# The tokens of each expert pair gathered by two fp32r matmul passes in place of one fp32 pass, in a fused two-block transformer kernel

## The chip, the cores and the metric

One core of a Trainium2 chip runs the whole kernel. The metric is device time in microseconds (us) for one execution. TensorE is called PE below, its weight loads PEld, VectorE DVE, ScalarE ACT, GpSimd POOL, and SyncE, which issues nearly all loads, SP.

## The reference, cut to what matters

Two transformer blocks in a row on 256 tokens of width 1024, all in float32. The first ends in a mixture of experts: every token picks one of 4 groups and two of the group's 4 experts.

```
g_sel = argmax(t @ w_rg + b_rg)                       # one group a token
top_p, top_i = top_k(softmax(e_logits[g_sel]), 2)     # two experts in it
combine[t, g, e] = one_hot(g_sel) * g_w * within      # 256 x 4 x 4, 2 nonzero a row
hid = silu(t @ w_gate[e]) * (t @ w_up[e])             # 1024 -> 512, 16 experts
y   = sum_e (hid * combine[:, e]) @ w_down[e]         # 512 -> 1024
```

The second block is a gated mixer with attention and a convolutional feed-forward part of width 2816; the change doesn't touch its arithmetic.

## The kernel before, in words

The kernel runs as one program, in this order: modulation and attention of block 1, its output projection, the router, eight steps over pairs of experts (`for p in range(8)`), a branch for the rare case that an expert has more than 64 tokens, and block 2. The order of PE's instructions is the order in which the code is written; the other engines are ordered by a scheduler.

**Number formats on PE.** A matmul of float32 operands stands in the trace as two records, each with a weight load of its own. Most products of the kernel are made instead from operands that are split into a high and a low part of type fp32r (`halves`, `mm3`, L332 to L334): a matmul of fp32r operands is one record with one weight load. For the experts' own matrices the kernel uses float32 (L1072, L1073, L1118, L1119).

**The expert step.** An expert's tokens are put into 64 slots. `slots_of` (L980 to L985) makes the 0/1 matrix `SS[p]` of a pair on DVE: for each of two blocks of 128 tokens a row per token, and 2 x 64 slots. `gather` (L1054 to L1062) multiplies it with the tokens: `hT` (tokens as rows, 1024 features, float32) gives the weights, 128 features at a time, and `SS[p]` the 128 moving columns. Eight feature tiles by two token blocks are 16 float32 matmuls a pair, which fill two PSUM banks. ACT and DVE in turn scale and shift each tile into `XE` (`affine`, L1050 and L1052). Then come, on PE: the gate matmuls (`pairmm(pg, 0)`, two experts beside each other in the two halves of the array's columns), two transposes of `SS[p]` and two small matmuls that fetch the combine weights (L1082, L1084), the up matmuls, `combine` of the pair before (L1027, L1028: fp32r, from `yH`, `yL` and the transposed 0/1 matrix `ST`), four transposes of the hidden values (L1106), the gather of the next pair, and the down matmuls. `gather(0)` stands ahead of the loop, right behind the router.

**Loads.** The expert matrices come as 96 chunks of 1 MB, in the order of their use, all on SP's queue (`moe_next`, L839 and L292). `KIND` names, for the first chunks in turn, the pool that lends the buffer: 0 `rawp`, 1 `big`, 2 `bigB`, 3 `wp`, 4 the tile `tL` of `ho`. The list has 21 entries, so 21 chunks can be on their way or unused at once; chunk n waits for the last reader of chunk n - 21. The first loads of block 2 (`in_wC`) follow on the same queue; `raw0` (L1169) is the first of them. It is split by ACT (L1176) and by DVE and POOL (L1179). At the branch (L1129) all engines meet.

Of the kernel before, what the change touches and what calls it, by code (L numbers as in the profile page):

```python
# [9 lines left out]
F32 = mybir.dt.float32  # L10
F32R = mybir.dt.float32r
I32 = mybir.dt.int32
AF = mybir.ActivationFunctionType
OP = mybir.AluOpType
# [3 lines left out]
P = 128  # L18
D = 1024
# [5 lines left out]
CAP = 64  # L25
# [91 lines left out]
LAG = 2  # L117
DELAY_FROM = NF - 2
LASTCUT = 94
KIND = [1] * 9 + [0, 0, 1, 0, 0, 2, 2, 2, 3, 3, 4, 1]  # L120
FIRST = "m0 m1 w0 w3"
WARM = 30
EARLY = ("x0 j4 g0 x1 r0 c0 s0 h0 pA g1 j1 c1 h1 pB A0 g2 A1 c2 h2 g3 B0 B1 c3 h3 A2 B2 pC g4 C0 C1 B3 c4 g5 h4 A3 C2 A4 c5 h5 B4 C3 g6 A5 c6 g7 h6 B5 C4 l0 A6 c7 h7 "
# [86 lines left out]
def build(tc, xT, cT, consts, constsA, constsZ, vec, wmod, wA, relb, wE, wC, sgw, sgb, sgln, gfin, out, dbg=None):  # L210
    nc = tc.nc
    vat = VEC_AT
    cat, catA, catZ = [c.at for c in _consts()]
    mm = nc.tensor.matmul
# [6 lines left out]
    with ExitStack() as top:  # L221
# [5 lines left out]
        wp = pool(top, "wp", bufs=WPB)  # L227
        pool(top, "gapH").tile([P, 16], F32, name="gapH")
        ho = pool(top, "ho")
# [31 lines left out]
        ident = cst("ident")  # L261
# [15 lines left out]
        def follow(d, e):  # L277
            tc.add_manual_dep(d.ins, e.ins.name, order_only, reason="first things first")
# [10 lines left out]
        def load(src, n=2048, pl=None, cuts=1):  # L289
            t = (pl or rawp).tile([P, 2048], F32, name=nm_("raw"), tag="raw")  # L290
            for a, b in pieces(n, cuts):
                queue(nc.sync.dma_start(t[:, a:b], src[:, a:b]))  # L292
            return t
# [69 lines left out]
        with ExitStack() as sa:  # L363
            ap = pool(sa, "ap")
            big = pool(sr, "big", bufs=BIG, side="right")

            def bigt(shape, name, dt=F32):
                n = int(np.prod(shape[1:]))
                t = big.tile([P, 2048], dt, name=name, tag="raw")
                t = t[:shape[0], :n]  # L370
                if len(shape) == 3:
                    return t.rearrange("p (a b) -> p a b", a=shape[1])
                if len(shape) == 4:
                    return t.rearrange("p (a b c) -> p a b c", a=shape[1], b=shape[2])
                return t
# [42 lines left out]
            with ExitStack() as sp:  # L418
# [14 lines left out]
                sqs_, d = [], silu  # L433
                for i, src in enumerate((X, CX)):
                    sq = bigt([P, KD, T], f"sq{i}")
                    sqs_.append(sq)
                    for k in range(0, KD, 2):
                        e = nc.scalar.activation(sq[:, k:k + 2], src[:, k:k + 2], AF.Square)
                        follow(e, d)
                        d = e  # L440
# [6 lines left out]
                col = pp.tile([P, 4], F32, name="colA")  # L447
# [81 lines left out]
                for step in EARLY.split():  # L529
                    f, k = step[0], step[1]  # L530
# [3 lines left out]
                    k = int(k)  # L534
# [66 lines left out]
                ps = proj(ch[1], 0, 512, 64)  # L601
# [227 lines left out]
            def moe_next():  # L829
                i = moe_q[0]  # L830
                moe_q[0] += 1
                n = i - len(KIND)
                kind = KIND[i % len(KIND)]
                if kind == 0:
                    return load(moe_chunk(i), cuts=2 if i >= LASTCUT else 1)
                pl, tag = {1: (big, "raw"), 2: (bigB[-1], "raw"), 3: (wp, "w"), 4: (ho, "tL")}[kind]
                t = pl.tile([P, 2048], F32, name=nm_("raw"), tag=tag)
                for a, b in pieces(2048, 2 if i >= LASTCUT else 1):
                    d = queue(nc.sync.dma_start(t[:, a:b], moe_chunk(i)[:, a:b]))  # L839
                    tc.add_manual_dep(d.ins, (used[n] if n >= 0 else moe_gate[0]).ins.name, complete, reason="prefetch")  # L840
                return t
# [81 lines left out]


        with sb:
            def small(shape, name, dt=F32):
                return bp.tile([P] + shape, dt, name=name)

            def bc(ap_, n):
                return ap_.unsqueeze(len(ap_.shape)).to_broadcast(list(ap_.shape) + [n])  # L930
# [14 lines left out]
            nc.vector.tensor_reduce(mx_, L, axis=AX.X, op=OP.max)  # L945
            nc.vector.tensor_sub(L, L, bc(mx_, 4))
            lexp[0] = nc.scalar.activation(ex, L, AF.Exp)
            hT = ho.tile([P, 2, D], F32, name="hT", tag="tH")
            for g in range(2):
                for b in range(2):  # L950
                    follow(nc.scalar.activation(hT[:, b, g * 512:(g + 1) * 512], tks[g, b], AF.Copy, scale=col[:, b:b + 1]), lexp[0])
            e1 = small([2, 5, 4], "e1")
            nc.vector.scalar_tensor_tensor(e1, L, 0.0, prio, op0=OP.is_ge, op1=OP.mult)
            nc.vector.tensor_reduce(mx_, e1, axis=AX.X, op=OP.max)
# [23 lines left out]
            SS = {}  # L978

            def slots_of(p):  # L980
                SS[p] = mix[:, 1536 + p % 2 * 256:1792 + p % 2 * 256].rearrange("p (b e s) -> p b e s", b=2, e=2)
                for b in range(2):
                    nc.vector.tensor_tensor(SS[p][:, b], bc(place[:, b, 2 * p:2 * p + 2], CAP),
                                            slot.unsqueeze(1).to_broadcast([P, 2, CAP]), op=OP.is_equal)
                SS[p] = SS[p].rearrange("p b e s -> p b (e s)")  # L985

            slots_of(0)
            comb = small([2, 4, 4], "comb")
            nc.vector.tensor_mul(comb, exe, top)
            den = small([2, 5], "den")  # L990
# [63 lines left out]
            def gather(p):  # L1054
                for g in range(2):
                    ps = bank()
                    for k in range(4):
                        for b in range(2):
                            d = (4 * g + k) * P
                            mm(ps[:, k * P:(k + 1) * P], hT[:, b, d:d + P], SS[p][:, b], start=b == 0, stop=b == 1)  # L1060
                    for k in range(4):
                        affine(XE[:, 4 * g + k], ps[:, k * P:(k + 1) * P], 4 * g + k, k % 2)  # L1062

            gather(0)
            for p in range(8):
# [13 lines left out]
                pairmm(pg, 0)  # L1079
                aux = bank()  # L1080
                for b in range(2):
                    nc.tensor.transpose(aux[:, b * P:(b + 1) * P], SS[p][:, b], ident)  # L1082
                for b in range(2):
                    mm(aux[:, 256:272], SS[p][:, b], comb[:, b], start=b == 0, stop=b == 1)  # L1084
                ST = br.tile([P, T], F32R, name=f"ST{p}", tag="ST")
                nc.vector.tensor_copy(ST, aux[:, :T])
                wt = br.tile([P, 1], F32, name=f"wt{p}", tag="wt")
# [39 lines left out]
                if p == 6:  # L1127
                    last[0] = None
                    with tc.If(n_most > CAP):  # L1129
                        spare = [bigB[-1].tile([P, 2048], F32, name=f"spare{c}", tag="raw") for c in range(3)]  # L1130
                        H2f, fw = spare[0].rearrange("p (k t) -> p k t", k=KD), spare[1:]
                        for k in range(KD):
                            ps = bank()
                            for b in range(2):
                                nc.tensor.transpose(ps[:, b * P:(b + 1) * P], hT[:, b, k * P:(k + 1) * P], ident)
                            affine(H2f[:, k], ps[:, :T], k, False)
                        hc = bigt([P, 5, T], "hc")
                        hid, cr = hc[:, 0:4], hc[:, 4]
                        with tc.For_i(0, NE, 1) as e:
                            nc.gpsimd.dma_start(cr, ovD[bass.ds(e, 1)].to_broadcast([P, T]))  # L1140

                            def dload(c):
                                t = fw[c % 2]
                                nc.sync.dma_start(t, wE[bass.ds(e, 1), c].rearrange("o p n -> p (o n)"))
                                return t
                            wg = [dload(0), dload(1)]
                            for f in range(4):
                                pg = bank()
                                for k in range(KD):
                                    s = slice((k % 4) * 512 + f * P, (k % 4) * 512 + (f + 1) * P)  # L1150
                                    mm(pg[:, :T], wg[k // 4][:, s], H2f[:, k], start=k == 0, stop=k == KD - 1)
                                nc.scalar.activation(hid[:, f], pg[:, :T], AF.Silu)
                            wu = [dload(2), dload(3)]
                            for f in range(4):
                                pu = bank()
                                for k in range(KD):
                                    s = slice((k % 4) * 512 + f * P, (k % 4) * 512 + (f + 1) * P)
                                    mm(pu[:, :T], wu[k // 4][:, s], H2f[:, k], start=k == 0, stop=k == KD - 1)
                                nc.vector.tensor_mul(hid[:, f], hid[:, f], pu[:, :T])
                                nc.vector.tensor_mul(hid[:, f], hid[:, f], cr)  # L1160
                            wd = [dload(4), dload(5)]
                            for m in range(KD):
                                ps = bank()
                                for f in range(4):
                                    s = slice((f % 2) * D + m * P, (f % 2) * D + (m + 1) * P)
                                    mm(ps[:, :T], wd[f // 2][:, s], hid[:, f], start=f == 0, stop=f == 3)
                                nc.vector.scalar_tensor_tensor(X[:, m], ps[:, :T], mod2[:, 24 + m:25 + m], X[:, m], op0=OP.mult, op1=OP.add)
            hH, hL = pairhl("z")
            pre = []  # L1169
            raw0 = load(wC[0], cuts=2)  # L1170
            hlast = list(ylast)

            def pre_high(i):
# [471 lines left out]
```

## Time and profile before

| | us |
|---|---|
| median of 3 runs | 788.2 (786.36 to 789.36) |
| the profiled execution | 787.9 |
| its span, first to last instruction | 786.3 |
| PE busy | 761.1 (97% of the span) |
| DVE, ACT, POOL busy | 451.9, 359.1, 28.2 |
| records of L1060 (gather) | 256, 31.6 us busy |

The profile is of one execution, 1.6 us longer than its span. A record's length is not its cost on a pipelined engine: what it costs is the distance from its start to the next record's start. "Idle before" counts the time in which an engine stood still, with what ended it.

### The profile page before, as it was taken

Reading aid. Unit: us, or ns where it says so; the run is one execution under the profiler, and the core shown is the slowest. Engines: PE = TensorE matmul, PEld = TensorE weight load, DVE = VectorE, ACT = ScalarE, POOL = GpSimd, SP = SyncE. Lnnn points to the kernel's source line nnn. Section 1 sums busy time; section 2 is a strip of 40 time slices with the busy share of each in tenths; the row PEclk is TensorE's granted clock in tenths of the full one; section 3 lists DMA queues with packets and bytes.
Section 4 is the critical chain, followed back from the end, with each engine's and each line's share of the span. In section 5 each row is a group of like instructions: output and inputs, shape, how many; then the busy total and the mean of one; then the engine's idle time right before and its main releaser. Section 6 shows DMA issues by size and latency. Waiting matters only on the chain. (4 is left out here: it accounts for less than half of the span.)

```text
span 786.3 us, 12554 instructions
## 1 busy us (share of the span) xinstructions
PE 761.1 (97%) x5022; PEld 561.9 (71%) x5022; DVE 451.9 (57%) x926; ACT 359.1 (46%) x669; POOL 28.2 (4%) x35
## 2 busy tenths in 40 slices
PE   8999998999998999999999989999999999999996
PEld 7577786766788445535535535898799999999995
DVE  3736628865764123313313325897877878787785
ACT  5426335675663211111102105578775755655654
POOL 0001000000002000000000003203000000000000
PEclk9899999999999999999999999999999999999998
DMA  8766636657959899999999926744333555545301
GB/s 358 303 269 139 263 134 248 221 200 259 420 183 351 333 415 421 419 419 419 419 421 419 416 99 231 268 161 161 134 133 142 210 168 215 206 165 208 111 1 54
DMA packets 29342, 198.86 MB, mean 253 GB/s; under 512 B 3456, under 2 KB 3856, under 8 KB 6368
## 3 DMA queue, kind: packets, MB, share of 16 engines
q1 hardware_dynamic: 28224, 194.45, 64.0%
q0 software_dynamic: 1056, 3.56, 2.0%
q8 instruction: 41, 0.67, 0.3%
q14 instruction: 21, 0.17, 0.1%
HBM read 196.94 MB, written 1.06 MB: 252 GB/s over the span
## 5 line engine op out<-in xcount | busy, mean ns | idle before, releaser
L313 DVE TENSOR_TENSOR w<-raw,w 128x1024 fp32r<-128x1024 f32 (+1 forms) x118 | 139.9, 1213 | 29.8 <-ACT w L312 29.7
L312 ACT CAST w<-raw 128x1024 fp32r<-128x1024 f32 (+1 forms) x118 | 116.5, 1029 | 22.8 <-PE b L334 20.6
L1072 PE MATMUL b<-raw,mix 128*64 128x512 f32 x256 | 114.7, 601 | 2.2 <-DVEq L1129 2.2
L1073 PE MATMUL b<-raw,mix 128*64 128x512 f32 x256 | 114.7, 601 | 0.0
L334 PE MATMUL b<-fH,w 128*128 128x256 f32 x352 | 98.5, 280 | 0.0
L332 PE MATMUL b<-fH,w 128*128 128x256 f32 x352 | 98.4, 279 | 0.0
L333 PE MATMUL b<-fL,w 128*128 128x256 f32 x352 | 98.2, 279 | 0.0
L1072 PEld LDWEIGHTS b<-raw,mix 128*64 128x64 f32 x256 | 34.5, 138 | 71.6 <-issue 70.4
L333 PEld LDWEIGHTS b<-fL,w 128*128 128x128 f32 x352 | 66.2, 188 | 0.9
L332 PEld LDWEIGHTS b<-fH,w 128*128 128x128 f32 x352 | 65.9, 187 | 0.8
L334 PEld LDWEIGHTS b<-fH,w 128*128 128x128 f32 x352 | 66.0, 188 | 0.0
L1118 PE MATMUL b<-raw,mix 128*64 128x512 f32 x128 | 56.6, 595 | 0.0
L1119 PE MATMUL b<-raw,mix 128*64 128x512 f32 x128 | 56.6, 595 | 0.0
L1568 ACT ACTIVATE a<-t,V 128x256 f32<-128x256 f32 x44 | 26.3, 599 | 39.0 <-DVE t L1567 39.0
L1118 PEld LDWEIGHTS b<-raw,mix 128*64 128x64 f32 x128 | 16.9, 137 | 33.1 <-issue 32.0
L1107 ACT COPY mix<-b 128x256 f32<-128x256 f32 x16 | 5.4, 374 | 73.5 <-PE b L1106 73.3
L332 PE MATMUL b<-w,mH 128*128 128x512 f32 x88 | 34.9, 396 | 0.0
L1101 DVE SCALAR_TENSOR_TENSOR mix<-mix,wt,b 128x256 f32<-128x256 f32 x16 | 7.0, 477 | 48.4 <-PE b L1073 43.2
L333 PE MATMUL b<-w,mH 128*128 128x512 f32 x88 | 34.8, 395 | 0.0
L334 PE MATMUL b<-w,mL 128*128 128x512 f32 x88 | 34.8, 395 | 0.0
L1073 PEld LDWEIGHTS b<-raw,mix 128*64 128x64 f32 x256 | 34.5, 138 | 0.0
L1123 DVE TENSOR_TENSOR YY<-b,YY 128x512 fp32r<-128x512 f32 x16 | 10.9, 689 | 38.5 <-ACT YY L1123 38.5
(427 smaller groups left out, 1700.6 us busy)
## 6 DMA issues: line engine op xcount, KB each, us to landing
raw<-in_wE SPq DMA_DIRECT2D x94, 1024.0 KB, 13.7
raw<-in_wC SPq DMA_DIRECT2D x46, 1024.0 KB, 4.9
raw<-in_wmod SPq DMA_DIRECT2D x24, 1024.0 KB, 6.1
raw<-in_wA SPq DMA_DIRECT2D x13, 1024.0 KB, 5.0
raw<-in_wE SPq DMA_DIRECT2D x4, 512.0 KB, 17.0
raw<-in_wA SPq DMA_DIRECT2D x2, 576.0 KB, 4.8
X<-in_xT SPq DMA_DIRECT2D x1, 1024.0 KB, 4.8
CX<-in_cT SPq DMA_DIRECT2D x1, 1024.0 KB, 7.3
```

The costliest lines, as they stand in the source:

```text
L312: hc = nc.scalar.copy(h[:, : b - a], raw[:, a:b])
L313: after[0] = (on or nc.vector).tensor_sub(l[:, : b - a], raw[:, a:b], h[:, : b - a])
L332: mm(ps, ah, bh, start=start, stop=False)
L333: mm(ps, ah, bl, start=False, stop=False)
L334: mm(ps, al, bh, start=False, stop=stop)
L1072: la = mm(ps[0:64], XE[:, k, 0:64], wa[:, s], start=k == 0, stop=k == KD - 1)
L1073: lb = mm(ps[64:128], XE[:, k, 64:128], wb[:, s], start=k == 0, stop=k == KD - 1)
L1101: nc.vector.scalar_tensor_tensor(sg[:, o], sg[:, o], wt, pu[:, o], op0=OP.mult, op1=OP.mult)
L1118: la = mm(pd[n][0:64], hd[:, f, 0:64], wa[:, s], start=f == 0, stop=f == 3)
L1119: lb = mm(pd[n][64:128], hd[:, f, 64:128], wb[:, s], start=f == 0, stop=f == 3)
L1123: ylast = (nc.scalar.copy(yH[:, o], pd[n]), nc.vector.tensor_sub(yL[:, o], pd[n], yH[:, o]))
L1568: nc.scalar.activation(a, t, AF.Identity, bias=bcv[:, n:n + 1], scale=wcv[:, 2, n:n + 1])
```

## The change

The tokens are now kept as two fp32r tiles: `hTH` is the old `hT` rounded to fp32r by ACT, `hTL` the remainder, made by four new DVE instructions from the same PSUM banks. `SS[p]` is an fp32r tile in a pool of its own with one buffer (it was a part of `mix`, with two in turn). `gather` runs over `hTH` and then `hTL` for each bank: 32 fp32r matmuls a pair in place of 16 float32 ones. The transposes and small matmuls of L1082 and L1084 stay as they were, on the same bits read as float32. `hTL` takes the tile `tL`, so `KIND` loses its entry 4 and has 20. `SS` takes a new tile in `br`; to make room, the router's small float32 tiles move into the freed columns of `mix`, and `raw0` and the branch's spare tiles come from `big`.

```
-KIND = [1] * 9 + [0, 0, 1, 0, 0, 2, 2, 2, 3, 3, 4, 1]
+KIND = [1] * 9 + [0, 0, 1, 0, 0, 2, 2, 2, 3, 3, 1]
...
-            hT = ho.tile([P, 2, D], F32, name="hT", tag="tH")
+            hTH = ho.tile([P, 2, D], F32R, name="hTH", tag="tH")
+            hTL = ho.tile([P, 2, D], F32R, name="hTL", tag="tL")
             for g in range(2):
                 for b in range(2):
-                    follow(nc.scalar.activation(hT[:, b, g * 512:(g + 1) * 512], tks[g, b], AF.Copy, scale=col[:, b:b + 1]), lexp[0])
+                    follow(nc.scalar.activation(hTH[:, b, g * 512:(g + 1) * 512], tks[g, b], AF.Copy, scale=col[:, b:b + 1]), lexp[0])
...
             def slots_of(p):
-                SS[p] = mix[:, 1536 + p % 2 * 256:1792 + p % 2 * 256].rearrange("p (b e s) -> p b e s", b=2, e=2)
+                st = br.tile([P, 256], F32R, name=f"SS{p}", tag="SS", bufs=1)
+                SS[p] = st.bitcast(F32).rearrange("p (b s) -> p b s", b=2), st.rearrange("p (b s) -> p b s", b=2)
...
-            slots_of(0)
+            placed = slots_of(0)
+            for g in range(2):
+                for b in range(2):
+                    o = slice(g * 512, (g + 1) * 512)
+                    placed_ = nc.vector.scalar_tensor_tensor(hTL[:, b, o], tks[g, b], col[:, b:b + 1], hTH[:, b, o], op0=OP.mult, op1=OP.subtract)
+                    follow(placed_, placed)
+                    placed = placed_
...
             def gather(p):
                 for g in range(2):
                     ps = bank()
-                    for k in range(4):
-                        for b in range(2):
-                            d = (4 * g + k) * P
-                            mm(ps[:, k * P:(k + 1) * P], hT[:, b, d:d + P], SS[p][:, b], start=b == 0, stop=b == 1)
+                    for i, ht in enumerate((hTH, hTL)):
+                        for k in range(4):
+                            for b in range(2):
+                                d = (4 * g + k) * P
+                                mm(ps[:, k * P:(k + 1) * P], ht[:, b, d:d + P], SS[p][1][:, b], start=i + k + b == 0, stop=i + k + b == 5)
...
-            raw0 = load(wC[0], cuts=2)
+            raw0 = load(wC[0], pl=big, cuts=2)
```

On PE, at `gather(0)` behind the router, before (a row is an instruction, `x8` eight alike in a row; `b` is a PSUM bank, out<-in):

```order
L973 MATMUL b_2506<-sel,C 128x32
L974 MATMUL b_2506<-sel,ones 128x16
L1060 MATMUL b_2528<-mix,hT 128x128 x8
L1060 MATMUL b_2541<-mix,hT 128x128 x8
L1072 MATMUL b_2554<-raw_1812,mix 64x512
L1073 MATMUL b_2554<-raw_1830,mix 64x512
```

and now:

```order
L981 MATMUL b_2498<-mix,C 128x32
L982 MATMUL b_2498<-mix,ones 128x16
L1076 MATMUL b_2521<-SS_2502,hTH 128x128 x8
L1076 MATMUL b_2521<-SS_2502,hTL 128x128 x8
L1076 MATMUL b_2542<-SS_2502,hTH 128x128 x8
L1076 MATMUL b_2542<-SS_2502,hTL 128x128 x8
L1088 MATMUL b_2563<-raw_1812,mix 64x512
L1089 MATMUL b_2563<-raw_1830,mix 64x512
```

Twice eight float32 matmuls become four times eight of fp32r; nothing else moves on PE here.

On DVE, at the same place, before:

```order
L976 SCALAR_TENSOR_TENSOR place<-sel,b_2506 128x32
L995 TENSOR_TENSOR cw<-den,oh 128x8
L983 TENSOR_TENSOR mix<-place,C 128x128 x2
L996 TENSOR_TENSOR cw<-cw,den 128x8
L997 TENSOR_TENSOR comb<-comb,cw 128x32
L1050 TENSOR_SCALAR mix<-b_2528,G_2262,mod_99 128x128 x2
```

and now (`place`, `cw`, `comb` have become columns of `mix`):

```order
L984 SCALAR_TENSOR_TENSOR mix<-mix,b_2498 128x32
L1010 TENSOR_TENSOR mix<-mix 128x8
L992 TENSOR_TENSOR SS_2502<-mix,C 128x128 x2
L1000 SCALAR_TENSOR_TENSOR hTL<-b_2431,mix,hTH 128x512
L1000 SCALAR_TENSOR_TENSOR hTL<-b_2436,mix,hTH 128x512
L1000 SCALAR_TENSOR_TENSOR hTL<-b_2441,mix,hTH 128x512
L1000 SCALAR_TENSOR_TENSOR hTL<-b_2446,mix,hTH 128x512
L1011 TENSOR_TENSOR mix<-mix 128x8
L1012 TENSOR_TENSOR mix<-mix 128x32
L1065 TENSOR_SCALAR mix<-b_2521,G_2262,mod_99 128x128 x2
```

The four instructions for `hTL` stand right behind the 0/1 matrix of pair 0 and ahead of the rest of the combine weights and of the scaling of `gather(0)`.

On SP, at the end of the expert loads, before (`in_wE` the last expert chunks, `in_wC` block 2):

```order
L839 DMA raw_3516<-in_wE 128x1024 x2
L292 DMA raw_3930<-in_wC 128x1024 x2
L292 DMA raw_4078<-in_wC 128x2048
L1129 COMPARE_AND_BRANCH
...
L1129 UNCONDITIONAL_BRANCH
L292 DMA raw_4188<-in_wC 128x2048
```

and now:

```order
L839 DMA raw_3628<-in_wE 128x1024 x2
L1145 COMPARE_AND_BRANCH
...
L1145 UNCONDITIONAL_BRANCH
L292 DMA raw_4060<-in_wC 128x1024 x2
L292 DMA raw_4208<-in_wC 128x2048
L292 DMA raw_4318<-in_wC 128x2048
```

The first two loads of block 2, `raw0` among them, have moved from before the branch to behind it.

## Rows read from the trace of the kernel before

**Rows 1.** Page, busy us of each engine, and issues of block 2's loads.
```profile
PE 761.1 (97%) x5022; PEld 561.9 (71%) x5022; DVE 451.9 (57%) x926; ACT 359.1 (46%) x669; POOL 28.2 (4%) x35
...
raw<-in_wC SPq DMA_DIRECT2D x46, 1024.0 KB, 4.9
```
**Rows 2.** Waits of PE, whole span: who <- for whom: us, times, longest.
```profile
PE b L1072 <- DVEq L1129: 2.2, 1, 2.2
PE b L973 <- DVE sel L969: 2.1, 1, 2.1
...
PE b L1060 <- DVE mix L983: 0.7, 1, 0.7
```
**Rows 3.** Timeline of PE at pairs 0 and 1: start us, us, instruction.
```profile
252.73 5.44 PE L1060 MATMUL b<-mix,hT 128*128 128x128 f32 x32 [0.69 <-DVE mix L983]
258.10 0.64 PE L1072 MATMUL b<-raw,mix 128*64 128x512 f32 x1
...
274.33 3.74 PE L1060 MATMUL b<-mix,hT 128*128 128x128 f32 x32
278.00 0.64 PE L1118 MATMUL b<-raw,mix 128*64 128x512 f32 x1
```
**Rows 4.** Line L1060, eight gathers: ns min/median/max, first and last start.
```profile
L1060 PEld LDWEIGHTS b<-mix,hT x256: 186/192/338, 252.7 to 445.1; 128*128 128x128 f32 x128
L1060 PE MATMUL b<-mix,hT x256: 274/275/426, 252.7 to 445.2; 128*128 128x128 f32 x128
```
**Rows 5.** Windows, gather(0): stretch, us, busy of engines, PE clock, DMA.
```profile
252.70:258.10 5.40, 5.37 (x33) 5.28 (x33) 1.68 (x8) 0.92 (x2) 0.00 (x0) 0.68 1.00 423
```
**Rows 6.** Line L333, weight loads of fp32r: ns min/median/max.
```profile
L333 PEld LDWEIGHTS b<-fL,w x352: 187/188/192, 592.8 to 770.5; 128*128 128x128 f32 x176
...
L333 PEld LDWEIGHTS b<-zL,wfH x8: 87/88/88, 500.0 to 502.4; 128*8 128x8 f32 x8
```
**Rows 7.** Timeline of PEld: two fp32r loads, then float32 loads of one-column matmuls.
```profile
237.93 0.19 PEld L332 LDWEIGHTS b<-oH,whl 128*128 128x128 f32 x1
238.04 0.19 PEld L333 LDWEIGHTS b<-oL,whl 128*128 128x128 f32 x1
...
246.21 0.30 PEld L911 LDWEIGHTS b<-ones,mix 128*128 128x128 f32 x2
...
246.66 0.30 PEld L911 LDWEIGHTS b<-ones,mix 128*128 128x128 f32 x2
```
**Rows 8.** Timeline of PE: fp32r, 256 moving columns, weights of 8 columns.
```profile
500.69 0.28 PE L332 MATMUL b<-zH,wfH 128*8 128x256 f32 x1
...
501.70 0.28 PE L332 MATMUL b<-zH,wfH 128*8 128x256 f32 x1
```
**Rows 9.** Timeline of DVE: 0/1 matrices, first scaling; then block 1's last combine.
```profile
252.29 0.49 DVE L983 TENSOR_TENSOR mix<-place,C 128x128 f32<-128x128 f32 x2
...
256.66 0.41 DVE L1050 TENSOR_SCALAR mix<-b,G,mod 128x128 f32<-128x128 f32 x1 [3.07 <-ACT mix L1052]
...
483.04 3.22 DVE L1031 SCALAR_TENSOR_TENSOR X<-b,mod,X 128x256 f32<-128x256 f32 x8
```
**Rows 10.** Line L839, the last expert chunk in two cuts, issue and landing.
```profile
L839 SPq DMA_DIRECT2D raw<-in_wE x2: 328/328/328, 435.4 to 437.8; - x2
...
DMA to landing us min/median/max: 16.2/16.3/16.4
```
**Rows 11.** Timeline of PE: its first use, two down steps before the end.
```profile
478.14 0.59 PE L1118 MATMUL b<-raw,mix 128*64 128x512 f32 x1
```
**Rows 12.** Timeline of SP: first loads of block 2.
```profile
440.37 5.31 SPq L292 DMA_DIRECT2D raw<-in_wC  x3
...
473.16 22.60 SPq L292 DMA_DIRECT2D raw<-in_wC  x6
```
**Rows 13.** Timeline of ACT: their first use.
```profile
482.30 1.05 ACT L1176 CAST w<-raw 128x1024 fp32r<-128x1024 f32 x1
...
487.84 1.99 ACT L312 CAST w<-raw 128x1024 fp32r<-128x1024 f32 x2
```

More of the change, by code (lines that the diff above doesn't have):

```diff
@@ L835, in moe_next @@
                     return load(moe_chunk(i), cuts=2 if i >= LASTCUT else 1)
-                pl, tag = {1: (big, "raw"), 2: (bigB[-1], "raw"), 3: (wp, "w"), 4: (ho, "tL")}[kind]
+                pl, tag = {1: (big, "raw"), 2: (bigB[-1], "raw"), 3: (wp, "w")}[kind]
                 t = pl.tile([P, 2048], F32, name=nm_("raw"), tag=tag)
@@ L925, in build @@
         with sb:
+            taken = [1536]
             def small(shape, name, dt=F32):
-                return bp.tile([P] + shape, dt, name=name)
+                if dt != F32:
+                    return bp.tile([P] + shape, dt, name=name)
+                taken[0] += math.prod(shape)
+                assert taken[0] <= 2048
+                names = "abc"[:len(shape)]
+                return mix[:, taken[0] - math.prod(shape):taken[0]].rearrange(f"p ({' '.join(names)}) -> p {' '.join(names)}", **dict(zip(names[:-1], shape)))
             def bc(ap_, n):
@@ L980, in slots_of @@
             def slots_of(p):
-                SS[p] = mix[:, 1536 + p % 2 * 256:1792 + p % 2 * 256].rearrange("p (b e s) -> p b e s", b=2, e=2)
+                st = br.tile([P, 256], F32R, name=f"SS{p}", tag="SS", bufs=1)
+                SS[p] = st.bitcast(F32).rearrange("p (b s) -> p b s", b=2), st.rearrange("p (b s) -> p b s", b=2)
                 for b in range(2):
-                    nc.vector.tensor_tensor(SS[p][:, b], bc(place[:, b, 2 * p:2 * p + 2], CAP),
-                                            slot.unsqueeze(1).to_broadcast([P, 2, CAP]), op=OP.is_equal)
-                SS[p] = SS[p].rearrange("p b e s -> p b (e s)")
-            slots_of(0)
+                    d = nc.vector.tensor_tensor(SS[p][1][:, b].rearrange("p (e s) -> p e s", e=2), bc(place[:, b, 2 * p:2 * p + 2], CAP),
+                                                slot.unsqueeze(1).to_broadcast([P, 2, CAP]), op=OP.is_equal)
+                return d
+            placed = slots_of(0)
[5 more added lines that the diff above has]
+                    placed = placed_
             comb = small([2, 4, 4], "comb")
@@ L1081, in build @@
                 for b in range(2):
-                    nc.tensor.transpose(aux[:, b * P:(b + 1) * P], SS[p][:, b], ident)
+                    nc.tensor.transpose(aux[:, b * P:(b + 1) * P], SS[p][0][:, b], ident)
                 for b in range(2):
-                    mm(aux[:, 256:272], SS[p][:, b], comb[:, b], start=b == 0, stop=b == 1)
+                    mm(aux[:, 256:272], SS[p][0][:, b], comb[:, b], start=b == 0, stop=b == 1)
                 ST = br.tile([P, T], F32R, name=f"ST{p}", tag="ST")
@@ L1129, in build @@
                     with tc.If(n_most > CAP):
-                        spare = [bigB[-1].tile([P, 2048], F32, name=f"spare{c}", tag="raw") for c in range(3)]
+                        spare = [bigt([P, 2048], f"spare{c}") for c in range(3)]
                         H2f, fw = spare[0].rearrange("p (k t) -> p k t", k=KD), spare[1:]
+                        hR = fw[0].rearrange("p (b d) -> p b d", b=2)
+                        nc.vector.tensor_add(hR, hTH, hTL)
                         for k in range(KD):
@@ L1134, in build @@
                             for b in range(2):
-                                nc.tensor.transpose(ps[:, b * P:(b + 1) * P], hT[:, b, k * P:(k + 1) * P], ident)
+                                nc.tensor.transpose(ps[:, b * P:(b + 1) * P], hR[:, b, k * P:(k + 1) * P], ident)
                             affine(H2f[:, k], ps[:, :T], k, False)
```

## The prediction

> **What bounds the kernel now.** I read the page first: PE is busy for 761.1 of 786.3 us, every other engine for little more than half of the span or less [rows 1]. So an edit is worth what it takes from or adds to PE's own sequence; work on DVE, ACT or SP counts only where PE comes to wait for it. Then the waits of PE, where the reader is to see that the expert stage has hardly any: ahead of the first gather PE waits 2.1 and 0.7 us for the router's small DVE steps, and 2.2 us at the branch [rows 2]. Then PE's timeline at the gathers [rows 3], the durations of their line [rows 4], and the windows view of the first gather for its clock [rows 5]. Last come the loads: when the last expert chunk lands and is used, and when block 2's first matrices are issued and used [rows 10 to 13].
>
> **The gathers on PE.** A gather is now 16 float32 matmuls, that is 32 records with 32 weight loads; eight of them give the 256 of each in [rows 4]. The second one starts at 274.33, and the next line starts at 278.00: 3.67 us, of which 32 records a pitch of 0.112 apart are 3.58 [rows 3]. The first one takes 252.73 to 258.10 = 5.37 us, since PE had stood idle just before and the granted clock averaged 0.68 of full speed there, between the half and the full level [rows 3, 5]: 0.168 a record. After the change a gather is 32 fp32r matmuls, each one record with one load: again 32 records and 32 loads. What counts is whether the pitch of a record changes.
>
> It has two candidates for a limit, the weight load and the stream of the moving columns. The load: an fp32r load of 128 columns takes 187 ns and one of 8 columns 87 ns [rows 6], so 120 columns are 100 ns, 0.83 ns a column, 0.107 us for 128 columns if loads follow each other without a gap. They do follow each other nearly so: two fp32r loads of 128 columns start 0.11 us apart [rows 7]. Four float32 loads of matmuls with only one moving column take from 246.21 to 246.66, 0.1125 each [rows 7]; with next to nothing to stream, the load alone sets that pace. The stream: with weights of 8 columns, nine fp32r matmuls of 256 moving columns take 500.69 to 501.70, 0.112 each [rows 8], so 128 columns are about 0.056. The stream is half of the load and lies behind it; the load sets 0.112, and that is the pitch of today. Change of a gather: 32 x (0.112 - 0.112) = 0.
>
> No fp32r matmul with under 256 moving columns is in the trace, so I bound it. From below by the stream alone: 0.056, a gather of 1.79 us. From above by two float32 records of 128 columns, as if fp32r had no advantage at this size: 0.224, a gather of 7.17 us. I take 0.112, the value of the nearest rows, the loads of [rows 7], which have the same 128 columns and the same format.
>
> The Trainium skill, "TensorE: Matmul & The Clock Gate", section "Weight-path perf modes — Fast Weight Load (FWL) and DoubleRow", states that a fast load comes on by itself when there are 128 weights and the type isn't FP32. If it counted fp32r as another type than FP32, the sum would go by the lower bound; the trace speaks against that, since fp32r loads of 128 columns last 187 ns [rows 6] and float32 ones 192 [rows 4].
>
> **The remainder `hTL` on DVE.** Four new instructions of 128x512 from PSUM stand behind `SS[0]` and ahead of the first scaling. The nearest row has the same operation, from PSUM, with 256 columns: 3.22 us for eight, 0.40 each [rows 9]. So 512 columns are at most 0.80. `SS[0]` is done at 252.29 + 0.49 = 252.78 [rows 9], the four then at 253.6, 254.4, 255.2 and 256.0. PE starts with the eight matmuls on `hTH` and wants the first two remainders at its 9th and 10th matmul, 252.73 + 8 x 0.168 = 254.1 and 254.2, and the other two at the 25th and 26th, 256.8 and 256.9. That is a wait of 0.2 us at most. Should PE wait longer, its last eight matmuls still start at 256.0 and end at 256.9 by the full clock's pitch, before today's 258.1. The next step's inputs wait for PE anyway. DVE has 3.07 us of idle time just there [rows 9], so its scaling at 256.66 is not late. Bounds for the first gather: +0.2, and -1.3 should the short wait make nothing slower and the clock rise as early as it can. I take 0. The ACT instructions that make `hTH` are as many and as large as those of `hT`.
>
> **`SS` with one buffer.** `SS[p+1]` now has to wait for the transposes and small matmuls that read `SS[p]`. They run on PE behind the gate matmuls, and the next gather comes only after the up matmuls, the combine and the hidden transposes. Two short DVE steps (0.49 us for both [rows 9]) fit there. Cost 0.
>
> **The loads.** With 20 buffers in place of 21 each later chunk is issued one buffer later, a few microseconds (a 1 MB load alone lands in 4.9 us [rows 1]). Today the last chunk is issued at 435.4 and 437.8 and lands 16.4 us later, at 454.2 [rows 10]; its first use is at 478.14 [rows 11]. Of the 23.9 us of slack at least 19 are left, and no wait of PE in [rows 2] is for a load. Cost 0. What would be gone without this cover is the difference, one to one.
>
> Block 2's first loads move: `raw0` now waits for a buffer of `big`, and stands on SP's queue behind the branch, with the second matrix behind it. Today they go out at 440.37 [rows 12]. The branch is passed by about 455, and the buffers that they take were read by the matmuls of pair 6 and the up matmuls of pair 7. So `raw0` goes out at about 455 and lands some 5 us later, at 460; ACT first wants it at 482.30 [rows 13], 22 us to spare. The second matrix goes out by 473.16, when the loads behind it go out today [rows 12], so it lands by 478.1, and is wanted at 487.84 [rows 13], 9.7 to spare. Cost 0. The branch itself and its 2.2 us stay.
>
> **The sum.** The profiled execution took 787.9 us, 0.3 below the median of the runs, 788.2. Gathers 0, remainder 0 (+0.2 to -1.3), `SS` 0, loads 0. I forecast 788.0, no change; a measurement of this kernel can tell about 0.5%, 3.9 us, from no change. The likeliest case's own range is 784.5 to 791.5.
>
> **Rivals.** *The stream sets the pitch.* If the load could hide or were quicker for this use, a matmul would cost 0.056: 32 x 0.056 = 1.8 us less a gather, 14.3 us over eight, 774. For it: fp32r streams a column in half the time of a float32 record's. Against it: the loads of [rows 6, 7], as long and as far apart as float32's. The loads of the chunks would not stop it, with 19 us of slack. The fast load rule of the Trainium skill (same page and section) would come out here; by the trace's 187 ns I give it no more. Chance 0.05.
>
> *Slower: fp32r has no advantage at 128 moving columns.* If the array takes at this size as long as for the two float32 records, the pitch is 0.224 and a gather 7.17 us: 3.58 more, times eight 28.7, 816. Its place is the new line of `gather`, and it decides from the point where such a matmul costs more than the 0.112 of its load. A part of it, load and stream one after the other (0.168), would give 32 x 0.056 x 8 = +14, 802. For it: no row shows fp32r at fewer than 256 moving columns. Against it: for 256 columns the cost is 0.112 in all, and less work should not cost more. Chance 0.10.
>
> *Slower: block 2's first matrix is late.* If its buffer came free only with the last down matmuls of block 1, near 481.6, `raw0` would land 4.9 later, at 486.5, 4.2 after ACT wants it: 792. It decides as soon as the landing passes 482.30. For it: it now stands behind the branch in a shared pool. Against: the buffers in question were read several us earlier. Chance 0.03.
>
> **How the numbers follow.** The forecast holds 0.82, the rivals 0.05, 0.10 and 0.03. Of the forecast's 0.82, 0.02 each go to small effects that come out past 0.5% on either side, as many short waits of DVE or ACT that move together. Faster: 0.05 + 0.02 = 0.07; slower: 0.10 + 0.03 + 0.02 = 0.15; same: 0.78. The range from 784.5 to 792.0 takes in the likeliest case and the late matrix, some 8 in 10; the ends at 774, 802 and 816 stay outside.
>
> **What would show it.** In the new profile a gather is a row of 32 fp32r matmuls that lasts about 3.7 us until the next line starts, with loads near 190 ns. Gathers of 1.8 us would show the first rival, of 5.4 or 7.2 the second. The remainder's four rows on DVE should end before 256.1, with a PE wait for them under 0.3 us. No wait of PE in the expert stage should name a load; a wait of ACT for the first `in_wC` load near 482 would show the third rival. The span stays within 4 us of 786.3, or the forecast is wrong.

## The result, and the profile after

The changed kernel takes 791.5 us in the median of 6 runs, the kernel before 787.4 in runs beside it: ratio 1.0057, 95% interval 1.004 to 1.0073. That is 4.0 us slower by the medians and 4.5 by the ratio. The forecast was 788.0 and no change. The time lies inside the range, but the sign of the change is clear and was not forecast.

The profiled execution took 791.35 us with a span of 789.7, 3.4 more than the span of before. Busy time on the page of the changed kernel:

```profile
PE 764.5 (97%) x5022; PEld 564.1 (71%) x5022; DVE 454.6 (58%) x930; ACT 359.0 (45%) x669; POOL 28.1 (4%) x35
```

PE has as many records as before and 3.4 us more of busy time [rows 1]. So it isn't a wait. The waits of PE are the old ones, in the same order (us in total, times, longest), with no load among them [rows 2]:

```profile
PE b L1088 <- DVEq L1145: 2.2, 1, 2.2
PE b L981 <- DVE mix L977: 2.1, 1, 2.1
...
PE b L1076 <- DVE SS L992: 0.7, 1, 0.7
```

Then PE's timeline (start us, us, instruction), first at pair 1, then at pair 0:

```profile
278.12 1.09 PE L1076 MATMUL b<-SS,hTH 128*128 128x128 f32 x8
...
281.82 0.64 PE L1134 MATMUL b<-raw,mix 128*64 128x512 f32 x1
```
```profile
253.35 1.53 PE L1076 MATMUL b<-SS,hTH 128*128 128x128 f32 x8 [0.70 <-DVE SS L992]
254.68 1.91 PE L1076 MATMUL b<-SS,hTL 128*128 128x128 f32 x8
...
258.09 1.91 PE L1076 MATMUL b<-SS,hTL 128*128 128x128 f32 x8
259.93 1.12 PE L1088 MATMUL b<-raw,mix 128*64 128x512 f32 x1
...
263.40 1.01 PE L1088 MATMUL b<-raw,mix 128*64 128x512 f32 x1
...
264.25 0.59 PE L1088 MATMUL b<-raw,mix 128*64 128x512 f32 x1
...
264.68 0.59 PE L1088 MATMUL b<-raw,mix 128*64 128x512 f32 x1
```

At pair 1 the gather takes 281.82 - 278.12 = 3.70 us; before it took 3.67 [rows 3]. At pair 0 it takes 6.58 against 5.37 [rows 3], and behind it the first five steps of the expert matmuls are 0.85 to 0.91 us apart, where the sixth takes 264.68 - 264.25 = 0.43. Everything from 254 to 264 runs at half speed. The windows of PE over that place (stretch, length, busy time, granted clock, DMA share and GB/s) say it outright:

```profile
252.00:254.00 2.00, 1.27 (x9) 1.00 1.01 426
254.00:258.00 4.00, 4.00 (x21) 0.50 0.88 369
...
260.00:264.00 4.00, 4.00 (x10) 0.50 0.00 0
264.00:265.00 1.00, 1.00 (x6) 0.88 0.00 0
265.00:268.00 3.00, 3.00 (x16) 1.00 0.37 79
253.30:264.60 11.30, 11.25 (x44) 0.55 0.38 158
```

The granted clock has two levels, 1.2 and 2.4 GHz, so a mean of m over a stretch means the lower level for (1 - m) / 0.5 of it: here (1 - 0.55) x 11.3 / 0.5 = 10.2 us. Before it was there for (1 - 0.68) x 5.40 / 0.5 = 3.5 us [rows 5], and came back inside the first gather. A us at half clock costs half a us: 5.1 against 1.7, a difference of 3.4 us. That is the whole difference of the two profiled spans.

### The profile page after: what moved, and what is told of

Its sections match the earlier page's. It is cut to its first block, busy times and chain, and to the rows that moved or that the text cites. A ratio compares the mean times of both kernels' runs of the same rounds, so it can differ in the third digit from the quotient of the medians.

```text
span 789.7 us, 12550 instructions
## 1 busy us (share of the span) xinstructions
PE 764.5 (97%) x5022; PEld 564.1 (71%) x5022; DVE 454.6 (58%) x930; ACT 359.0 (45%) x669; POOL 28.1 (4%) x35
## 5 line engine op out<-in xcount | busy, mean ns | idle before, releaser
L1088 PE MATMUL b<-raw,mix 128*64 128x512 f32 x256 | 116.8, 611 | 2.2 <-DVEq L1145 2.2
L1089 PE MATMUL b<-raw,mix 128*64 128x512 f32 x256 | 116.8, 611 | 0.0
L333 PE MATMUL b<-fL,w 128*128 128x256 f32 x352 | 98.3, 279 | 0.0
L333 PEld LDWEIGHTS b<-fL,w 128*128 128x128 f32 x352 | 65.9, 187 | 0.9
L1134 PE MATMUL b<-raw,mix 128*64 128x512 f32 x128 | 56.6, 595 | 0.0
L1135 PE MATMUL b<-raw,mix 128*64 128x512 f32 x128 | 56.6, 595 | 0.0
L1102 DVE CAST ST<-b 128x256 fp32r<-128x256 f32 x8 | 3.4, 425 | 55.7 <-PE b L1100 55.7
L333 PE MATMUL b<-w,mH 128*128 128x512 f32 x88 | 34.7, 394 | 0.0
```

The costliest lines, as they stand in the source:

```text
L333: mm(ps, ah, bl, start=False, stop=False)
L1088: la = mm(ps[0:64], XE[:, k, 0:64], wa[:, s], start=k == 0, stop=k == KD - 1)
L1089: lb = mm(ps[64:128], XE[:, k, 64:128], wb[:, s], start=k == 0, stop=k == KD - 1)
L1134: la = mm(pd[n][0:64], hd[:, f, 0:64], wa[:, s], start=f == 0, stop=f == 3)
L1135: lb = mm(pd[n][64:128], hd[:, f, 64:128], wb[:, s], start=f == 0, stop=f == 3)
```

## The experiments

Theory A: behind the router's waits the clock falls in both kernels; the float32 gather brings it back, the fp32r gather does not, and the clock returns only behind the expert matmuls. Theory B: the clock returns when it does, whatever PE runs, and the time is lost in the rest of the change (`hTL`, the buffers, the loads).

**Pair 0 back in float32.**

```diff
-                    for i, ht in enumerate((hTH, hTL)):
+                    for i, ht in enumerate((hTH, hTL) if p else ()):
...
+                    for k in range(0 if p else 4):
+                        for b in range(2):
+                            d = (4 * g + k) * P
+                            mm(ps[:, k * P:(k + 1) * P], hTH.bitcast(F32)[:, b, d:d + P], SS[p][0][:, b], start=b == 0, stop=b == 1)
```

> The changed kernel with gather(0) alone made of 16 float32 matmuls over hTH (for pair 0 the low part is left out); hTL is still made, pairs 1 to 7 stay in fp32r. Theory A (the clock): behind the router's waits the clock falls to half; a float32 gather brings it back within some 3.5 us, the fp32r gather does not. It expects gather(0) at about 5.4 us instead of 6.6, the clock at half for about 3.5 us instead of 10.2, and some 3.4 us less than the changed kernel: 788. Theory B (the clock comes back when it does, whatever PE runs; or the time is lost in hTL or the buffers) expects the 10.2 us at half clock and the 791.5 us of the changed kernel.

Measured: 787.7 us, ratio to before 1.0004 (0.999 to 1.0018). PE's timeline there:

```profile
253.36 5.44 PE L1080 MATMUL b<-SS,hTH 128*128 128x128 f32 x32 [0.70 <-DVE SS L992]
258.73 0.64 PE L1092 MATMUL b<-raw,mix 128*64 128x512 f32 x1
```

and the windows:

```profile
253.00:257.00 4.00, 3.64 (x21) 0.67 1.01 424
257.00:261.00 4.00, 4.00 (x25) 0.91 0.17 70
```

The gather starts where the changed kernel's does, at 253.36, takes 5.37 us, and the clock is back by 258. One gather of eight carries the loss. The rest of the change is still in this kernel, though pair 0 doesn't read its `hTL`, and costs nothing that shows; theory B falls.

**The mirror: pairs 1 to 7 in float32.** The same edit with its condition turned round.

```diff
-                    for i, ht in enumerate((hTH, hTL) if p else ()):
+                    for i, ht in enumerate((hTH, hTL) if p == 0 else ()):
...
-                    for k in range(0 if p else 4):
+                    for k in range(4 if p else 0):
```

> The mirror: gather(0) in fp32r as in the changed kernel, pairs 1 to 7 with 16 float32 matmuls over hTH (their low part is left out). Theory A expects the changed kernel's time, 791.5, within 0.5 us, since at the full clock both gathers take 3.7 us, and half clock for 10 us behind the router. The rival that each fp32r gather costs 0.5 us more than a float32 one expects 788.

Measured: 791.7 us, 1.0049 (1.0031 to 1.0068), as theory A expects. The clock's windows are those of the changed kernel:

```profile
253.00:257.00 4.00, 3.44 (x19) 0.68 1.00 424
257.00:261.00 4.00, 4.00 (x18) 0.50 0.17 70
261.00:265.00 4.00, 4.00 (x14) 0.54 0.00 0
```

So the seven later gathers cost the same in either type, within the interval.

**The waits filled.** Matmuls that nobody reads go onto PE ahead of the rank matmuls (L981) and ahead of `gather(0)`.

```diff
+            fil = bank()
+            XF = X[:, 0:2].rearrange("p k t -> p (k t)")
+            for _ in range(5):
+                mm(fil[:, :512], ones, XF, start=True, stop=True)
             rk = bank()
...
+            for _ in range(2):
+                mm(fil[:, :512], ones, XF, start=True, stop=True)
             gather(0)
```

> The changed kernel with float32 matmuls of 512 columns that nobody reads put on PE into the two router waits: 5 ahead of L981, 2 ahead of gather(0). Theory A expects the clock not to fall there: gather(0) 3.6 us instead of 6.6, the first L1088 lines at full clock, about 5.1 us less, minus up to 0.5 for matmuls that end after the wait: 786.5 to 787. If the idle time is not what lowers the clock: 791.5 to 792.

Measured: 787.4 us, 1.0001 (0.9988 to 1.0014). The clock stayed full, but the fillers were too long, as PE's timeline shows:

```profile
249.34 4.46 PE L983 MATMUL b<-X,ones 128*128 128x512 f32 x10
...
255.40 1.41 PE L1080 MATMUL b<-SS,hTH 128*128 128x128 f32 x8
```

I had counted 0.43 us for a float32 matmul of 512 columns; it is 0.43 for each of its two records. The gather starts at 255.40 instead of 253.35, 2.05 late. The 786.5 to 787 expected are missed by the length of the fillers; the next two runs have shorter ones.

**Smaller fillers, on both kernels** (four of 256 columns, then one; the edit is against the one above).

```diff
-            XF = X[:, 0:2].rearrange("p k t -> p (k t)")
-            for _ in range(5):
-                mm(fil[:, :512], ones, XF, start=True, stop=True)
+            XF = X[:, 0]
+            for _ in range(4):
+                mm(fil[:, :T], ones, XF, start=True, stop=True)
...
-            for _ in range(2):
-                mm(fil[:, :512], ones, XF, start=True, stop=True)
+            for _ in range(1):
+                mm(fil[:, :T], ones, XF, start=True, stop=True)
```

> The changed kernel with smaller fillers in the two router waits: 4 float32 matmuls of 256 columns ahead of L981 (8 records of 0.21, 1.7 of the 2.1 us) and 1 ahead of gather(0) (0.43 of the 0.7 us). The first fillers overran by 2.05 us. Theory A expects no fall of the clock and no overrun: about 2 us less than those, 785.3.

> The kernel before with the same fillers. Theory A expects the half-clock stretch of 3.5 us to go, 1.7 us of loss, so about 786; and the same time within 1 us as the changed kernel with fillers, since without the fall of the clock the two gathers cost the same.

Measured: 785.2 us for the changed kernel, 0.9983 (0.997 to 0.9996), and 785.7 for the kernel before, 0.9989 (0.9975 to 1.0003). In both, every window around the gather has the full clock; first the changed kernel's, then those of the kernel before:

```profile
250.00:253.00 3.00, 2.61 (x15) 1.00 1.02 421
253.00:257.00 4.00, 3.68 (x29) 1.00 1.01 426
257.00:261.00 4.00, 4.00 (x23) 1.00 0.15 64
```
```profile
253.00:257.00 4.00, 3.83 (x33) 1.00 1.01 426
257.00:261.00 4.00, 4.00 (x21) 1.00 0.76 317
```

With the clock kept, the two kernels take the same time: the change itself is worth nothing that shows, and what it loses is the clock's. The fp32r gather doesn't lower the clock either: here it runs at the full level from start to end.

The fillers give the changed kernel 6.3 us, more than the 5.1 that half clock cost it at the router. The rest is at another place. At the branch PE waits some 2 us in every kernel here (2.2 in these). Behind that wait the clock is at its lower level for some 3.4 us, 1.7 us lost, in the profiled executions of the kernel before, of the changed one and of the two with one type for pair 0 and the other for the rest; in those of all the others it stays full there. The windows of PE behind it, in the changed kernel without and with the smaller fillers:

```profile
458.00:462.00 4.00, 3.94 (x12) 0.60 0.81 273
```
```profile
454.00:458.00 4.00, 4.00 (x20) 1.00 0.87 275
```

No filler stands near the branch; why the clock holds there was not tried. For the kernel before the gain of the fillers is not clear of the noise.

**A gather of two pairs with 256 moving columns.** Theory A leaves open what it is in the fp32r gather: the type, or that each matmul streams 128 columns behind a load that takes as long as 256. The same question asks for a better kernel, since a load is paid per matmul.

```diff
-KIND = [1] * 9 + [0, 0, 1, 0, 0, 2, 2, 2, 3, 3, 1]
+KIND = [1] * 9 + [0, 0, 0, 0, 2, 2, 2, 3, 3]
...
-        XE = mix[:, :KD * P].rearrange("p (k s) -> p k s", k=KD)
+        XE = bigt([P, KD, 256], "XE")
+        SSw = bigt([P, 512], "SSw", F32R)
...
-                                mm(ps[:, k * P:(k + 1) * P], ht[:, b, d:d + P], SS[p][1][:, b], start=i + k + b == 0, stop=i + k + b == 5)
+                                mm(ps[:, k * 256:(k + 1) * 256], ht[:, b, d:d + P], SS[p][1][:, b], start=i + k + b == 0, stop=i + k + b == 3)
...
-                if p < 7:
+                if p % 2 and p < 7:
                     slots_of(p + 1)
                     gather(p + 1)
```

Not shown here: the 0/1 matrix is made for two pairs at a time, the gather fills four banks, and each pair reads its half of `XE`.

> The changed kernel with one gather for two pairs: the 0/1 matrix has 256 columns, so a gather is 32 fp32r matmuls with 256 moving columns, four gathers in place of eight; 18 chunk buffers in place of 20 (XE and the 0/1 matrix take the two). At full clock the load sets 0.112 for 128 columns and the stream 0.112 for 256, so a gather of two pairs should cost 3.6 us as one of a pair does: 14.4 us less. If it is the fp32r type that leaves the clock low, gather(0) takes 7.2 us at half clock and the clock comes back some 4 us after it: 777. If it is that an fp32r matmul of 128 columns streams for only half of the time, the clock comes back in gather(0) as with float32: 774. A load wait of PE near the end of the expert stage, for want of the two buffers, would give it back: up to 5 us.

Measured: 776.0 us, 0.9853 (0.9831 to 0.9875), some 12 us faster than the kernel before. PE's timeline of the gather for pairs 2 and 3, first and last part:

```profile
302.03 0.72 PE L1080 MATMUL b<-SSw,hTH 128*128 128x256 f32 x4
...
305.31 0.62 PE L1080 MATMUL b<-SSw,hTL 128*128 128x256 f32 x4
305.85 0.64 PE L1138 MATMUL b<-raw,mix 128*64 128x512 f32 x1
```

305.85 - 302.03 = 3.82 us for two pairs, where the changed kernel pays 3.70 for each. So the stream did not set the pitch at 128 columns: twice as much of it costs next to nothing. That the weight load set it fits its records (188 ns here, 192 in the changed kernel), and nothing else that is paid once a matmul was tried apart from it. For the clock the run is inconclusive. It lies between the two forecasts, and in the windows the clock had fallen earlier, ahead of the gather:

```profile
248.00:250.00 2.00, 2.00 (x14) 0.67 1.02 422
250.00:254.00 4.00, 2.08 (x10) 0.50 1.00 420
254.00:258.00 4.00, 3.97 (x17) 0.50 0.21 88
258.00:260.00 2.00, 2.00 (x15) 0.77 0.00 0
```

No long wait stands ahead of that fall. From 245.6 on PE runs float32 matmuls of 20 and of one moving column and then transposes, and its longest idle time there is 0.22 us, as in the kernels in which the clock holds at this place:

```profile
246.37 0.62 PE L897 MATMUL b<-mix,X 128*128 128x20 f32 x4 [0.22 <-DVE X L855]
```

In this kernel, then, theory A's router waits are not what the clock fell behind.

**Only the stream of `gather(0)` doubled.**

```diff
+                                    mm(ps[:, k * 256:(k + 1) * 256].rearrange("p (r s) -> p r s", r=2), ht[:, b, d:d + P],
+                                       SS[p][1][:, b].unsqueeze(1).to_broadcast([P, 2, P]), start=i + k + b == 0, stop=i + k + b == 3)
```

These lines stand in a loop of their own for pair 0, over four banks; only the first copy of the 128 slots goes into `XE`.

> The changed kernel with gather(0) alone over 256 moving columns: the 128 of SS[0] are read twice in a row, 32 fp32r matmuls into four banks, and the second copies are not used. Type, operands and number of loads are those of the changed kernel; only the stream is twice as long. If the fp32r type as such leaves the clock low (theory A1), the clock stays at half for some 10 us and the time is the changed kernel's or a little more, 791 to 792. If it is the short stream of an fp32r matmul of 128 columns (theory A2), the clock comes back within some 3.5 us and gather(0) takes 5.4 us or so: 788, as with float32.

Measured: 787.8 us, 1.0013 (0.9998 to 1.0029). The windows:

```profile
253.00:257.00 4.00, 3.82 (x18) 0.57 1.01 426
257.00:261.00 4.00, 4.00 (x27) 1.00 0.04 16
```

and PE's timeline:

```profile
253.16 1.20 PE L1077 MATMUL b<-SS,hTH 128*128 128x256 f32 x4 [0.70 <-DVE SS L992]
...
256.86 0.64 PE L1077 MATMUL b<-SS,hTH 128*128 128x256 f32 x4
...
258.85 0.64 PE L1099 MATMUL b<-raw,mix 128*64 128x512 f32 x1
```

Half clock for (1 - 0.57) x 4 / 0.5 = 3.4 us, and a gather of 258.85 - 253.16 = 5.69. With twice the columns, half of them useless, the kernel is 3.6 us faster than the changed one by the medians. It isn't the type: fp32r matmuls with the same weights (in another order) bring the clock back when they stream 256 columns. The other executions agree: all 12 of this kernel have a mean granted clock of 0.985 or more, all six of the changed one 0.983 or less.

**The two improvements together.**

> The gather of two pairs with 256 moving columns and the same fillers. Theory A expects gather(0) at 3.6 us instead of 6.5 and no half clock in the router: 3 to 5 us less than wide_gather's 776.0, so 771 to 773.

Measured: 774.1 us, 0.9835 (0.9812 to 0.9858), 12 to 13 us faster than the kernel before, and 1.9 less than without fillers. The expected 771 to 773 is missed: in its windows the clock is low already at 248, ahead of the fillers, and stays so until about 251.4 (0.17 x 4 / 0.5 = 1.4 us of the second window).

```profile
248.00:250.00 2.00, 2.00 (x11) 0.50 1.02 381
250.00:254.00 4.00, 4.00 (x21) 0.83 0.89 356
254.00:258.00 4.00, 3.42 (x24) 1.00 0.38 160
```

The edits are the 256-column gather and the smaller fillers above. Why the clock falls earlier in the profiled executions of these two kernels was not tried. Nor were fillers of fp32r with 128 columns.

## Why the prediction was wrong

**The step that failed** is the first gather's own term: "Bounds for the first gather: +0.2, and -1.3 [...] I take 0." It took over the 0.168 us a record of [rows 3, 5] and let the clock return at the same point with fp32r matmuls as with float32 ones; the bounds allowed only an earlier return. The runs show +1.2 us in `gather(0)` and half clock from 259.93 to about 264.2 behind it, another 2.1: with the rounding the 3.4 us of the spans. The prediction had the two numbers from which a doubt could have come: the stream of 128 fp32r columns is 0.056 of the 0.112 between two matmuls, and the clock was just then at its lower level. It drew from them that the stream is hidden, and not that PE's work differs from float32's at the one place where the clock had still to rise. No rival was about the clock; all three were about pitch or loads. That the time still lies inside the range is luck: the range was made for the scatter of a measurement and for a late matrix, and neither moved the time.

**The steps that held, and one that did not.** The pitch: 3.70 against the forecast 3.67 at full clock. Its loads are as long as float32's:

```profile
L1076 PEld LDWEIGHTS b<-SS,hTL x128: 192/192/333, 254.6 to 448.5; 128*128 128x128 f32 x128
```

A fast weight load of fp32r, which the Trainium skill's page "TensorE: Matmul & The Clock Gate", section "Weight-path perf modes — Fast Weight Load (FWL) and DoubleRow", would allow by the words of its trigger, isn't seen: 192 ns here, 192 for float32 [rows 4]. The remainder on DVE:

```profile
253.32 2.72 DVE L1000 SCALAR_TENSOR_TENSOR hTL<-b,mix,hTH 128x512 fp32r<-128x512 f32 x4
```

2.72 us for four, 0.68 each, under the bound of 0.80, and done at 256.0. At half clock PE doesn't wait for it. At full clock it does: in the changed kernel with the smaller fillers,

```profile
253.56 1.17 PE L1080 MATMUL b<-SS,hTH 128*128 128x128 f32 x8 [0.17 <-DVE SS L996]
254.57 0.27 PE L1080 MATMUL b<-SS,hTL 128*128 128x128 f32 x1
254.99 1.00 PE L1080 MATMUL b<-SS,hTL 128*128 128x128 f32 x7
...
257.71 0.64 PE L1094 MATMUL b<-raw,mix 128*64 128x512 f32 x1
```

the second matmul over `hTL` starts 0.42 us after the first, and the gather takes 4.15 us instead of 3.7. The widened gather with fillers names what it waits for:

```profile
255.91 0.62 PE L1084 MATMUL b<-SSw,hTL 128*128 128x256 f32 x3 [0.28 <-DVE hTL L1007]
```

The forecast had 0.2 at most. It set the time at which PE wants `hTL` by 0.168 us a matmul, the pace of a gather that is partly at half clock. The loads: the first of block 2 goes out behind the branch,

```profile
457.52 16.46 SPq L292 DMA_DIRECT2D raw<-in_wC  x4
```

and ACT takes it at 485.75 without a wait for it. `SS` with one buffer, 18 or 20 chunk buffers: no wait of PE names a load. None of the three rivals came.

## What to carry to other kernels

Where PE has been idle, ask at which clock the next matmuls run and what they do before it rises: two forms of the same product that cost the same at full clock can differ behind a wait. A matmul whose weight load is longer than its stream is worth widening, since more moving columns are nearly free and the same work then needs fewer loads. A few useless matmuls in a wait can pay where the clock falls behind it, if they end before the wait does: 6.3 us on the changed kernel, nothing clear of the noise on the one before.

## What was not expected of the hardware

PE's records fill 11.25 of 11.30 us from 253.30 on, and the clock is at its lower level for 10.2 of them. The Trainium skill, "TensorE: Matmul & The Clock Gate", section "What's actually happening", says that the clock follows how busy PE has been lately; the runs agree in direction, but a busy share of 100% in the profile does not show that PE was busy in this sense. Seen ahead of a rise were float32 gathers, expert matmuls, and fp32r matmuls with 256 moving columns; not seen in `gather(0)` was one behind fp32r matmuls with 128.

Executions of one kernel differ too. The kernel with the doubled stream took 786.4 to 786.8 us in the four with a mean granted clock of 0.990, and 787.2 to 789.4 in the eight with 0.985 to 0.987. Its profiled execution is one of the four, and the clock holds behind the branch; that of the kernel before has 0.987, and the clock falls there, 1.7 us lost. So a fall that comes in some executions and not in others is the likely difference, and it bears on every comparison of medians above. That it is the difference is not shown: one execution of each kernel was profiled.
